# Two gate tiles moved from attention into the stick breaking, and one gate's sigmoid written as exp and reciprocal

## The chip, the cores and the metric

The kernel runs on one core of a Trainium2 chip. The metric is the time of one execution in microseconds, device time. A time without a profile is a median of runs; a profile is one further execution, and its numbers are compared with that execution's own time.

The core has five engines that work side by side, each through its own list of instructions in order: PE (matrix products and transposes), DVE and ACT (element by element work, ACT also functions such as exp), POOL (element by element work) and SP, which here only issues loads and stores. An instruction waits for the ones whose results or whose buffers it needs, and everything behind it on its engine waits with it.

## What is computed

Two layers of a model over 512 tokens with 1024 features. Each layer has a mixer and a convolutional feed-forward part, each between two normalizations and added to the stream. The change touches the mixer:

```python
def hybrid_mixer(h, positions, w_in, ...):
    q_nsa, kv_nsa, g_nsa, qkv_sb, g_merge = jnp.split(h @ w_in, cuts, axis=-1)
    ...
    o_nsa = nsa_attention(...)
    o_sb = stick_breaking_attention(qkv[:, :, 0], qkv[:, :, 1], qkv[:, :, 2]).reshape(B, T, SB_WIDTH)
    g_a, g_b = jnp.split(jax.nn.sigmoid(g_merge), 2, axis=-1)
    y = g_a * (o_nsa @ w_proj_nsa) + g_b * (o_sb @ w_proj_sb)
    return y @ w_out

def stick_breaking_attention(q, k, v):
    ...
        z = jnp.einsum('bqhd,bkhd->bhqk', q[:, q0:q1], k[:, :q1]).astype(jnp.float32) * scale
        log_1m = jnp.where(strict, -jax.nn.softplus(z), 0.0)
        later = lax.cumsum(log_1m, axis=3, reverse=True) - log_1m
        w = jnp.where(strict, jnp.exp(jax.nn.log_sigmoid(z) + later), 0.0)
        outs.append(jnp.einsum('bhqk,bkhd->bqhd', w.astype(v.dtype), v[:, :q1]))
```

So the mixer needs, from one large product with `w_in`, the inputs of two attentions, and two gates of 1024 features each, `g_a` and `g_b`. The gates are used only after the attentions.

## The kernel before

Activations lie with features on the 128 partitions and tokens along the columns. Every number of a product is split into a high and a low part, and a product of 512 columns is three matmuls per 128 features (high with high, low with high, high with low): one output tile of 128 features is 24 matmuls, called a **tile of filling** here. Its weights come from a fixed list of items (`Weights`, in the order of the `it(...)` calls): SP loads an item into one of three raw buffers, ACT copies its high part (`whi`, L119), and DVE or POOL, as the item says, subtracts to get the low part (`wlo`, L123). `get` takes the next item, so the order of the list must be that of the tiles.

A mixer runs in two stages that matter here.

**Attention** (L888 to L1067). 32 pairs of head and query block (`Sub`) go through scores `S` on PE, maximum and small reciprocal on DVE (`st`, L955, L970, L971), exp on ACT (`P`), scaling on POOL (L974), transposes on PE (`tp`, L985, two banks), evacuation of the transposed weights as high part by ACT (`pt`, L994) and low part by DVE (L996), and the product with the values (`pv`). Behind these the program has the filling: four tiles for the queries and keys of the first two pairs of stick-breaking heads (`sb_pair`), eight tiles of the gate `ga` (`gate`, each evacuated by DVE at L849), and four tiles of values (`sb_values`: a tile, four transposes at L868 and an evacuation). A planner puts these matmuls among attention's instructions by its own estimates of durations; the result is fixed before the kernel runs. The filling has one accumulation bank here (`f`).

**Stick breaking** (L1073 to L1194). Eight heads, each in three steps: `s` (scores into a bank `Z`, then Abs, Exp, Relu, Ln on ACT and four scans and a subtraction on DVE), `t` (Exp on ACT, ten transposes on PE, high part `wh` by ACT, low part `wl` by DVE), `p` (product with the values, then `pvl` on ACT and `o_s` on DVE, which frees `Z`, of which there are two). The order of PE's work is written out in `SB_ORDER`: `s3` is step s of head 3, and each `f` takes the next piece of `filling()`: the last four tiles of `sb_pair`, eight tiles of the gate `gb`, and eight projections of attention's output of 12 matmuls each, multiplied into `ga` at L1162. PE keeps exactly that order (`chained`); the filling alternates between two banks, `f` and `g`.

Before the stick breaking both halves of `ga` go through a sigmoid:

```python
            for i in range(2):
                act(ga[i], ga[i], AF.Sigmoid)
```

`act` loads a function table (L268) whenever the function is of another set than the last one. Exp and Ln are in one set, Sigmoid is in another. The two halves of `gb` go through Sigmoid after the stick breaking in the program's text.

Of the kernel before, what the change touches and what calls it, by code (L numbers as in the profile page):

```python
# [13 lines left out]
AF = mybir.ActivationFunctionType  # L14
OP = mybir.AluOpType
# [20 lines left out]
SB_H = 8  # L36

SB_ORDER = ("s0 f s1 f f t0 f p0 f s2 t1 f p1 f s3 t2 f p2 f s4 t3 f p3 f s5 t4 f p4 f s6 "
            "t5 f f p5 f s7 t6 f f p6 f t7 f p7")

ALL = slice(0, T)
HALVES = (slice(0, HT), slice(HT, T))
# [148 lines left out]
def run_kernel(ctx, tc, xT, pos, inv, vec, pew, cw1, w_m, w_vn, w_pr, w_o, w_u, w_d, xmid, rot, out):  # L191
    nc = tc.nc
    uid = [0]

    def nm(s):
        uid[0] += 1
        return f"{s}_{uid[0]}"
# [11 lines left out]
    def hold(tag):  # L209
        return lambda i: held["slot"](tag, f"wh{i}", FR)  # L210
# [3 lines left out]
    def it(ap, n=1024, dest=None, eng=nc.vector, fold=0):  # L214
        items.append((ap, n, dest, eng, fold))

    for l in range(DEPTH):
        for i in range(HEAD):
            it(w_m[l, i], dest=hold(("sa", "sb", "vs0", "vs1")[i - 2]) if i >= 2 else None, eng=nc.vector)
        for c, n, k in ((0, 840, "q1"), (840, 840, "on"), (1680, 560, "sa")):  # L220
            it(w_vn[l, :, c:c + n], n, dest=hold(k))
        it(w_m[l, 6])
        it(w_m[l, 7])
        for v in range(2):
            it(cw1[l, :, v * 1024:(v + 1) * 1024], dest=hold(("vs0", "vs1")[v]), fold=16)
        for i in list(range(8, 12)) + list(range(16, 24)) + list(range(32, 36)):
            it(w_m[l, i], eng=nc.vector if i in (8, 9, 10) else nc.gpsimd)
        for i in list(range(12, 16)) + list(range(24, 32)):
            it(w_m[l, i])
        for i in range(8):  # L230
            it(w_pr[l, i])
        for i in range(8):
            it(w_o[l, i], dest=hold(("q0", "k0", "k1", "vs1")[i - 2]) if 2 <= i < 6 else None)
        for i in range(2 * NF):
            it(w_u[l, i], dest=hold(("sa", None, None, "q0", "k0", "k1")[i]) if i in (0, 3, 4, 5) else None)
        dts = list(range(8 - TAIL_D)) + 2 * list(range(8 - TAIL_D, 8))
        for j, i in enumerate(dts):
            k0 = 0
            for c, n in enumerate(DCH):
                keep = i == KEPT and c < 2  # L240
                if not (keep and j >= 8):
                    it(w_d[l, i, :, k0 * 128:(k0 + n) * 128], n * 128,
                       dest=(Strips(lambda: h_hi, 4 * c), Strips(lambda: h_lo, 4 * c)) if keep else None)
                k0 += n
# [7 lines left out]
    def after(op, earlier):  # L252
        tc.add_manual_dep(op.ins, earlier.ins.name,
                          mybir.DependencyInfo(mybir.DependencyClass.NoSync, mybir.DependencyReason.DATA),
                          reason="order of issue")

    def act(out_, in_, fn, **kw):


        load_table(fn)  # L260
        op = nc.scalar.activation(out_, in_, fn, **kw)  # L261
        after(op, table["load"])
        table["users"].append(op)

    def load_table(fn):
        name = SETS.get(fn, fn)
        if name != table["set"]:
            load = nc.scalar.preload_act_table_set(name) if isinstance(name, str) else nc.scalar.preload_act_table(fn)  # L268
            for op in table["users"]:
                after(load, op)  # L270
            table.update(set=name, load=load, users=[])
# [154 lines left out]
    def fbank(name):  # L426
        return ps1.tile([128, T], F, name=nm(name), tag="f" if name == "f" else "g", bufs=1)

    def gemm(o, wt, rhi, rlo, kts, first=True, last=True, woff=0, step=6, ahead=None):

        hi, lo = wt
        n = 0
        for j, kt in enumerate(kts):
            c = (woff + j) * 128
            a = hi[:, c:c + 128]
            b = lo[:, c:c + 128]
            f = first and j == 0
            e = last and j == len(kts) - 1
            for w_, r_, f_, e_ in ((a, rhi(kt), f, False), (a, rlo(kt), False, False), (b, rhi(kt), False, e)):
                mm(o, w_, r_, f_, e_)  # L440
                n += 1
                if n % step == 0 and not (e_ and last):
                    yield
        if ahead is not None:
            W.ensure(W.n_got - 1 + ahead)
        yield

    def drain(g, side=None):
        for _ in g:
            if side is not None:  # L450
                side.tick()

    def h_of(tr):
        return (lambda kt: h_hi[:, kt, tr]), (lambda kt: h_lo[:, kt, tr])
# [111 lines left out]
    for l in range(DEPTH):  # L566
# [8 lines left out]
        def slot(k, name, dt=F):  # L575
            return rp.tile([128, SLOT], dt, name=nm(name), tag=k)
# [236 lines left out]
        def fill_bank():  # L813
            fills[0] += 1
            return fbank("fg"[fills[0] % fills[1]])

        def sb_pair(p, st):

            st = st.rearrange("p (a e t) -> p a e t", a=2, e=2)
            qlo = rp.tile([128, T], FR, name=nm("qlo"), tag="qlo", bufs=4)  # L820
            for t in range(2):
                b = fill_bank()
                drain(gemm(b, W.get(), *h_of(ALL), range(KD), ahead=2))
                with tc.high_priority():
                    z = rp.tile([128, T], F, name=nm("sbz"), tag="sbz")
                    nc.vector.scalar_tensor_tensor(z, b, 0.125 if t == 0 else 1.0, r2, op0=OP.mult, op1=OP.mult)  # L826
                    for e in range(2):
                        r = slice(e * 64, e * 64 + 64)
                        ro = slice(64 - e * 64, 128 - e * 64)
                        d = st[:, t, e]  # L830
                        nc.scalar.copy(d[r], z[r])
                        if t == 0:
                            nc.sync.dma_start(d.bitcast(F)[ro], d.bitcast(F)[r])
                        nc.vector.tensor_sub(qlo[r] if t == 0 else d[ro], z[r], d.bitcast(F)[r])
                if t == 1:
                    sbq[p] = (st[:, 0], qlo, st[:, 1])
                yield

        ga, gb = {}, {}
        at = lambda s, k: s[k // 4][:, (k % 4) * T:(k % 4) * T + T]  # L840

        def gate(dst, half, tag):

            dst[half] = slot(tag, "gate")
            for m in range(4 * half, 4 * half + 4):
                b = fill_bank()
                drain(gemm(b, W.get(), *h_of(ALL), range(KD), ahead=2))
                with tc.high_priority():
                    nc.vector.tensor_mul(at(dst, m), b, r2)  # L849
                yield  # L850
# [6 lines left out]
        def sb_values():  # L857

            vS.extend([slot("q0", "vS0", FR), slot("k0", "vS1", FR)])
            for c in range(4):  # L860
                b = fill_bank()
                drain(gemm(b, W.get(), *h_of(ALL), range(KD), ahead=2))
                z = rp.tile([128, T], F, name=nm("sbz"), tag="sbz")
                with tc.high_priority():
                    nc.vector.tensor_mul(z, b, r2)
                tp = fbank("f")
                for j in range(4):
                    nc.tensor.transpose(tp[:, j * 128:(j + 1) * 128], z[:, j * 128:(j + 1) * 128], ident)  # L868
                with tc.high_priority():
                    src = tp.rearrange("p (j h c) -> p h j c", j=4, h=2)  # L870
                    v4 = vS[c // 2].rearrange("p (h j c) -> p h j c", h=4, j=4)[:, c % 2 * 2:c % 2 * 2 + 2]
                    nc.scalar.copy(v4[:, :, :, 0:64], src)
                    nc.vector.tensor_sub(v4[:, :, :, 64:128], src, v4.bitcast(F)[:, :, :, 0:64])
# [14 lines left out]
        with temps(0) as nt, pool("pn", space=PSUM) as pn:  # L888
# [173 lines left out]
                    pv_pair(pv_due.pop(0))  # L1062
            drain(sb_pair(0, slot("sa", "sbst", FR)))
            drain(sb_pair(1, slot("sb", "sbst", FR)))
            drain(gate(ga, 0, "vs0"))
            drain(gate(ga, 1, "vs1"))
            sb_values()  # L1067

# [2 lines left out]
        with temps(3) as sw, pool("pz", space=PSUM) as pz:  # L1073
# [91 lines left out]
            def filling():  # L1165
                yield from sb_pair(2, slot("vn", "sbst", FR))
                yield from sb_pair(3, sw.tile([128, SLOT], FR, name=nm("sbst")))
                yield from gate(gb, 0, "k1")
                yield from gate(gb, 1, "sa")
                yield from projection_n()  # L1170

            for i in range(2):
                act(ga[i], ga[i], AF.Sigmoid)
            heads = [Head(h) for h in range(SB_H)]
            fill = filling()
            fills[1] = 2
            chained[0] = True
# [253 lines left out]
```

## Time and profile before

| what | value |
|---|---|
| median of 3 runs | 1635.32 us (1633.79 to 1635.38) |
| the profiled execution | 1636.58 us, its span 1634.9 us |
| granted TensorE clock, mean | 0.985 |
| ACT_TABLE_LOAD (L268) | 20, 1283 ns each |
| first layer: scores S, and Z | 80.9 to 219.2 us, 245.3 to 382.2 us |
| second layer: scores S, and Z | 886.3 to 1024.3 us, 1050.7 to 1187.8 us |

The two layers run the same program in these stages, so one layer is read closely and counted twice. The views used are: the page's head with each engine's busy time; windows, which give the busy time of each engine in stretches of the span, with the clock that PE was granted; the waits of one engine, by what ended them; the chain of waits, followed back from the last instruction, in order of time; and rows of groups of like instructions with their mean durations. A matmul's own duration (0.39 us for 512 columns) overlaps the next one; what a tile of filling costs PE is read from the chain, where the pieces follow each other.

### The profile page before, as it was taken

How to read it: one execution, taken by the hardware profiler on the slowest of the kernel's cores; microseconds unless marked ns; L12 is line 12 of the kernel's file. 1: busy time of each engine (PE TensorE's matmuls, PEld its weight loads, DVE VectorE, ACT ScalarE, POOL GpSimd, SP SyncE). 2: the span in 40 equal slices, each digit the busy share in tenths (PEclk: the TensorE clock that was granted, in tenths of full speed). 3: DMA queues.
4: the chain of work that ended last, by engine and by line, in shares of the span. 5: the costliest groups of instructions: out<-in, count | busy, mean ns of one | idle time of the engine just before them, and what ended most of it. 6: DMA issues, size and time to landing. Idle time of an engine off the chain costs nothing. (4 is left out here: it accounts for less than half of the span.)

```text
span 1634.9 us, 23009 instructions
## 1 busy us (share of the span) xinstructions
PE 1585.0 (97%) x8874; PEld 1372.3 (84%) x8874; DVE 1095.1 (67%) x1671; ACT 887.9 (54%) x1412; POOL 182.8 (11%) x298
## 2 busy tenths in 40 slices
PE   9999999998999999999999999999799999999997
PEld 8878878876998888888998888787689988888897
DVE  8876666676578777733688766577576687776235
ACT  6865567664545444423568555666735454444232
POOL 0056440000000000000000655200000000000000
PEclk9999999998999999999999999999999999999999
DMA  6321112213412232333563211121143133323343
GB/s 224 115 75 43 53 39 91 65 52 116 142 53 91 90 104 90 100 94 112 170 201 88 72 40 52 43 89 64 51 168 103 40 103 93 101 95 93 98 129 119
DMA packets 50238, 153.66 MB, mean 94 GB/s; under 512 B 5584, under 2 KB 11216, under 8 KB 50128
## 3 DMA queue, kind: packets, MB, share of 16 engines
q1 hardware_dynamic: 47824, 146.23, 28.2%
q0 software_dynamic: 1296, 4.72, 0.8%
q8 instruction: 70, 1.15, 0.3%
q10 hardware_dynamic: 1008, 1.23, 0.3%
q14 instruction: 40, 0.33, 0.1%
HBM read 142.20 MB, written 4.72 MB: 90 GB/s over the span
## 5 line engine op out<-in xcount | busy, mean ns | idle before, releaser
L119 ACT CAST whi<-wraw 128x1024 fp32r<-128x1024 f32 (+2 forms) x227 | 233.1, 1028 | 307.0 <-PE bk L424 243.0
L123 DVE TENSOR_TENSOR wlo<-wraw,whi 128x1024 fp32r<-128x1024 f32 (+2 forms) x201 | 238.8, 1189 | 189.4 <-ACT whi L119 186.6
L424 PE MATMUL bk<-h_hi,wlo 128*128 128x512 f32 (+1 forms) x736 | 277.2, 377 | 0.0
L424 PE MATMUL bk<-h_hi,whi 128*128 128x512 f32 (+1 forms) x736 | 275.9, 375 | 0.6 <-ACT whi L119 0.6
L424 PE MATMUL bk<-h_lo,whi 128*128 128x512 f32 (+1 forms) x736 | 276.1, 375 | 0.0
L424 PE MATMUL f<-h_lo,whi 128*128 128x512 f32 (+1 forms) x416 | 163.5, 393 | 0.0
L424 PE MATMUL f<-h_hi,whi 128*128 128x512 f32 (+1 forms) x384 | 152.9, 398 | 7.5 <-DVE sbz L826 5.9
L424 PEld LDWEIGHTS bk<-h_hi,whi 128*128 128x128 f32 x736 | 138.3, 188 | 26.0 <-ACT whi L119 0.8
L424 PEld LDWEIGHTS bk<-h_hi,wlo 128*128 128x128 f32 x736 | 138.4, 188 | 25.3
L424 PEld LDWEIGHTS bk<-h_lo,whi 128*128 128x128 f32 x736 | 138.4, 188 | 24.7
L424 PE MATMUL f<-h_hi,wlo 128*128 128x512 f32 (+1 forms) x384 | 149.4, 389 | 0.0
L424 PE MATMUL bk<-ah,wlo 128*128 128x512 f32 (+1 forms) x420 | 142.6, 340 | 0.5 <-DVE wlo L123 0.5
L424 PE MATMUL bk<-ah,whi 128*128 128x512 f32 (+1 forms) x420 | 142.3, 339 | 0.0
L424 PE MATMUL bk<-al,whi 128*128 128x512 f32 (+1 forms) x420 | 142.2, 338 | 0.0
L974 POOL TENSOR_TENSOR P<-P,st 128x256 f32<-128x256 f32 x160 | 94.4, 619 | 108.8 <-DVE st L971 56.3
L1296 DVE TENSOR_TENSOR cu<-bk,r 128x512 f32<-128x512 f32 x88 | 60.2, 688 | 61.1 <-PE bk L424 60.9
L424 PE MATMUL bk<-h_hi,wh 128*128 128x256 f32 x512 | 95.9, 284 | 0.0
L424 PEld LDWEIGHTS f<-h_lo,whi 128*128 128x128 f32 x416 | 81.0, 195 | 13.1
L424 PEld LDWEIGHTS f<-h_hi,whi 128*128 128x128 f32 x384 | 73.8, 192 | 21.1 <-DVE sbz L826 6.3
L996 DVE TENSOR_TENSOR pt<-tp,pt 128x512 fp32r<-128x512 f32 (+1 forms) x96 | 56.3, 595 | 49.0 <-ACT pt L994 39.9
L424 PEld LDWEIGHTS bk<-ah,wlo 128*128 128x128 f32 x420 | 79.6, 190 | 9.4 <-DVE wlo L123 0.7
L424 PEld LDWEIGHTS bk<-ah,whi 128*128 128x128 f32 x420 | 79.7, 190 | 8.7
(261 smaller groups left out, 3384.1 us busy)
## 6 DMA issues: line engine op xcount, KB each, us to landing
wraw<-in_w_u SPq DMA_DIRECT2D x88, 512.0 KB, 3.5
wraw<-in_w_m SPq DMA_DIRECT2D x72, 512.0 KB, 3.3
wraw<-in_w_d SPq DMA_DIRECT2D x40, 512.0 KB, 3.5
wraw<-in_w_d SPq DMA_DIRECT2D x22, 384.0 KB, 3.0
wraw<-in_w_pr SPq DMA_DIRECT2D x16, 512.0 KB, 3.5
wraw<-in_w_o SPq DMA_DIRECT2D x16, 512.0 KB, 3.6
wraw<-in_cw SPq DMA_DIRECT2D x4, 512.0 KB, 3.7
kst<-kst SPq DMA_DIRECT2D x8, 256.0 KB, 3.4
```

What stands on the lines that cost most here:

```text
L119: self.nc.scalar.copy(hi[:, c], raw[:, c])
L123: eng.tensor_sub(lo[:, s], raw[:, s], hi.bitcast(F)[:, s])
L424: queue(nc.tensor.matmul(o, a, b, start=first, stop=last, skip_group_check=True))
L974: nc.gpsimd.tensor_mul(pv[:, j], pv[:, j], st[:, 2:4, None].to_broadcast([128, 2, 128]))
L996: nc.vector.tensor_sub(lo[:, :w_, self.hm], src, hi.bitcast(F)[:, :w_, self.hm])
L1296: nc.vector.tensor_mul(u, b, r2)
```

## The change

Attention's filling keeps six of the eight tiles of `ga`: two of the first half, then the values, then the other two of the first half and two of the second. The last two tiles of `ga` become pieces of the stick breaking's filling, after `sb_pair`. `SB_ORDER` has 22 `f` instead of 20, the new ones towards the end. The sigmoid of `ga` becomes `logistic`: Exp of the negative on ACT, then plus one and reciprocal on DVE, in place. The first half goes through it before the stick breaking, the second after its last tile. `gb` keeps its Sigmoid. The weights' list follows the new order; of the eight items of `ga` the six of attention's filling have POOL for the low part, and the last two DVE.

```diff
@@ SB_ORDER @@
-            "t5 f f p5 f s7 t6 f f p6 f t7 f p7")
+            "t5 f p5 f f s7 t6 f f p6 f f t7 f f p7")
@@ the items @@
-        for i in list(range(8, 12)) + list(range(16, 24)) + list(range(32, 36)):
+        for i in list(range(8, 12)) + [16, 17] + list(range(32, 36)) + list(range(18, 22)):
             it(w_m[l, i], eng=nc.vector if i in (8, 9, 10) else nc.gpsimd)
-        for i in list(range(12, 16)) + list(range(24, 32)):
+        for i in list(range(12, 16)) + list(range(22, 32)):
             it(w_m[l, i])
@@ behind attention @@
-            drain(gate(ga, 0, "vs0"))
-            drain(gate(ga, 1, "vs1"))
+            g0, g1 = gate(ga, 0, "vs0"), gate(ga, 1, "vs1")
+            next(g0)
+            next(g0)
             sb_values()
+            drain(g0)
+            next(g1)
+            next(g1)
@@ filling() of the stick breaking @@
                 yield from sb_pair(3, sw.tile([128, SLOT], FR, name=nm("sbst")))
+                yield from g1
+                logistic(ga[1])
                 yield from gate(gb, 0, "k1")
@@ ahead of the stick breaking @@
-            for i in range(2):
-                act(ga[i], ga[i], AF.Sigmoid)
+            def logistic(g):
+
+                act(g, g, AF.Exp, scale=-1.0)
+                nc.vector.tensor_scalar(g, g, 1.0, None, op0=OP.add)
+                nc.vector.reciprocal(g, g)
+
+            logistic(ga[0])
```

In the changed kernel the lines from L1063 on are shifted (L1126 is L1130, L1140 is L1144, L1151 is L1155, L1162 is L1166).

**Attention's tail on DVE**, second layer. `st` is a pair's maximum and its reciprocal, `pt<-tp,pt` the low part that frees a bank of transposes, `sbz` and `vS` belong to the values. Before:

```order
L996 TENSOR_TENSOR pt_9255<-tp_9302,pt_9254 128x2x128
L970 RECIPROCAL st_9340<-st_9340 128x2
L971 TENSOR_TENSOR st_9340<-st_9340,gates_7490 128x2
L873 TENSOR_TENSOR vS_1045_9948<-f_10029,vS_1045_9948 128x8x64
L996 TENSOR_TENSOR pt_9337<-tp_9326,pt_9336 128x4x128
L996 TENSOR_TENSOR pt_9339<-tp_9331,pt_9338 128x4x128
L970 RECIPROCAL st_9392<-st_9392 128x2
L971 TENSOR_TENSOR st_9392<-st_9392,gates_7490 128x2
```

And now, at the same pair of head and block (`gate_9662` is the first half of `ga`, `gate_9977` the second):

```order
L996 TENSOR_TENSOR pt_9251<-tp_9298,pt_9250 128x2x128
L970 RECIPROCAL st_9336<-st_9336 128x2
L971 TENSOR_TENSOR st_9336<-st_9336,gates_7486 128x2
L1181 TENSOR_SCALAR gate_9662<-gate_9662 128x2048
L1182 RECIPROCAL gate_9662<-gate_9662 128x2048
L996 TENSOR_TENSOR pt_9333<-tp_9322,pt_9332 128x4x128
L970 RECIPROCAL st_9388<-st_9388 128x2
L849 TENSOR_TENSOR gate_9977<-f_9978,r_90 128x512
```

Between the product of one pair and the low parts of the pair before it now stand the addition and the reciprocal over 128x2048. PE's list goes on, at that place, with the rest of a tile into bank f and then the transposes of the next pair, which go into the bank that `pt_9333<-tp_9322` frees.

**Attention's tail on ACT.** Before, a table load stands on each side of the two sigmoids, ahead of `pvl` and of the high parts `pt`:

```order
L261 ACTIVATE P_9402,st_9392<-S_9355,st_9392 128x4x128 x2
L268 ACT_TABLE_LOAD
L261 ACTIVATE gate_9666<-gate_9666 128x2048
L261 ACTIVATE gate_9807<-gate_9807 128x2048
L268 ACT_TABLE_LOAD
L1018 COPY pvl_9378<-pv_9361 64x256
L994 CAST pt_9336<-tp_9382 128x4x128
```

Now:

```order
L261 ACTIVATE P_9346,st_9336<-S_9316,st_9336 128x4x128 x2
L261 ACTIVATE gate_9662<-gate_9662 128x2048
L994 CAST pt_9332<-tp_9322 128x4x128
L261 ACTIVATE P_9398,st_9388<-S_9351,st_9388 128x4x128 x2
L994 CAST pt_9334<-tp_9327 128x4x128
L1018 COPY pvl_9374<-pv_9357 64x256
```

One Exp of the gate is left there, one pair earlier, and no load.

**The middle of the stick breaking on DVE.** `wl` is a head's low part (here of head 2), `sbr` the scans of head 3, `gate_10359` and `gate_10401` the first half of `gb`. Before:

```order
L1151 TENSOR_TENSOR o_s_10118<-Z_10194,pvl_10471 64x512
L849 TENSOR_TENSOR gate_10359<-g_10474,r_90 128x512
L123 TENSOR_TENSOR wlo_10500<-wraw_10340,whi_10499 128x1024
L1140 TENSOR_TENSOR wl_10542<-Z_10392,wh_10541 128x1280
L849 TENSOR_TENSOR gate_10359<-f_10545,r_90 128x512
L123 TENSOR_TENSOR wlo_10571<-wraw_10389,whi_10570 128x1024
```

Now:

```order
L1155 TENSOR_TENSOR o_s_10044<-Z_10119,pvl_10395 64x512
L1181 TENSOR_SCALAR gate_9977<-gate_9977 128x2048
L849 TENSOR_TENSOR gate_10401<-g_10402,r_90 128x512
L1182 RECIPROCAL gate_9977<-gate_9977 128x2048
L123 TENSOR_TENSOR wlo_10428<-wraw_10265,whi_10427 128x1024
L1144 TENSOR_TENSOR wl_10470<-Z_10316,wh_10469 128x1280
L849 TENSOR_TENSOR gate_10401<-f_10473,r_90 128x512
L123 TENSOR_TENSOR wlo_10499<-wraw_10313,whi_10498 128x1024
```

The second half's addition and reciprocal stand around a gate product, ahead of head 2's `wl`.

## The prediction

> **What bounds the kernel now.** The page's head and engine shares come first.
>
> ```profile
> span 1634.9 us, 23009 instructions
> PE 1585.0 (97%) x8874; PEld 1372.3 (84%) x8874; DVE 1095.1 (67%) x1671; ACT 887.9 (54%) x1412; POOL 182.8 (11%) x298
> ```
>
> PE is taken 97% of the span, so only two things move the time: PE work that goes, which this change hardly has, and the waits between PE's instructions. To find those I cut the second layer in four (the window view: length, then busy time of PE, PEld, DVE, ACT, POOL, granted clock): attention up to its last score block, attention's tail, the stick breaking until head 4 is out, and its end.
>
> ```profile
> 886.30:1024.30 138.00, 134.30 (x787) 113.08 (x785) 93.69 (x213) 81.71 (x211) 78.44 (x121) 0.99 0.16 54
> 1024.30:1050.70 26.40, 24.30 (x148) 21.01 (x145) 13.80 (x26) 17.46 (x27) 7.28 (x12) 0.94 0.11 41
> 1050.70:1140.10 89.40, 88.95 (x456) 73.79 (x455) 62.88 (x74) 63.88 (x66) 0.00 (x0) 1.00 0.23 77
> 1140.10:1187.70 47.60, 37.87 (x178) 30.60 (x176) 29.22 (x34) 29.37 (x26) 0.00 (x0) 0.89 0.15 45
> ```
>
> PE is full in the first and third stretch, and idle 9.7 us at the end of the stick breaking, where the clock drops as well. Who ends those waits, in the view of PE's waits from 1040 to 1190 (total, times, longest):
>
> ```profile
> PE Z L424 <- DVE wl L1140: 3.9, 2, 3.4
> PE Z L1136 <- ACT sbt L261: 3.7, 2, 2.8
> PE Z L424 <- DVE o_s L1151: 2.6, 2, 2.2
> ```
>
> All three are a head's softmax chain that PE has too little filling to cover. The chain of waits shows attention's tail (start, length):
>
> ```profile
> 1029.22 1.28 ACT L268
> 1030.52 3.14 ACT gate L261 x2
> 1034.26 1.28 ACT L268
> 1035.94 0.59 ACT pt L994
> 1037.40 1.09 PE tp L985 x4
> ```
>
> Two table loads and two sigmoids hold the evacuation of transposed weights there. So there is something to gain in both places; the question is what the new instructions on DVE cost. The prices, from the same chain, are those of one tile of filling, of a head's scores, its transposes, its output, and of half a tile (a projection):
>
> ```profile
> 1066.23 5.44 PE g L424 x24
> 1058.96 1.61 PE Z L424 x12
> 1071.67 1.09 PE Z L1136 x10
> 1078.27 1.17 PE Z L424 x8
> 1152.76 2.76 PE g L424 x12
> ```
>
> **The new DVE operations.** Each layer gets two reciprocals and two additions over 128x2048. The trace has reciprocals of 2 and of 16 columns only (min/median/max ns), and products of 16, 512 and 1024 columns:
>
> ```profile
> L970 DVE RECIPROCAL st<-st x64: 149/158/168, 89.6 to 1029.2; 128x2 f32<-128x2 f32 x64
> L913 DVE RECIPROCAL cm<-cm x4: 243/248/256, 108.7 to 973.3; 128x16 f32<-128x16 f32 x4
> L916 DVE TENSOR_TENSOR cm<-cm,gates 128x16 f32<-128x16 f32 x4 | 0.7, 168 | 0.0
> L1296 DVE TENSOR_TENSOR cu<-bk,r 128x512 f32<-128x512 f32 x88 | 60.2, 688 | 61.1 <-PE bk L424 60.9
> L123 DVE TENSOR_TENSOR wlo<-wraw,whi 128x1024 fp32r<-128x1024 f32 x177 | 216.4, 1223 | 144.6 <-ACT whi L119 141.9 <-PE bk L424 0.5
> L364 DVE TENSOR_SCALAR rt_n<-rt_ang 128x512 f32<-128x512 f32 x3 | 1.3, 422 | 0.0
> ```
>
> A product costs (1223 - 688)/512 = 1.045 ns a column, and at 16 columns still only 168 ns. The reciprocal takes 158 ns at 2 columns and 248 at 16, thus 90/14 = 6.4 ns a column. The bounds for 2048 columns: at the product's rate 0.15 + 2.14 = 2.3 us; by the widest reading of the two rows, (256 - 149)/14 = 7.6 ns a column, 15.8 us. I take the middle of the reciprocal's own rows, the nearest there are: 0.158 + 2046 x 6.43 ns = **13.3 us**. [...] The addition is 0.15 once and four times 0.27 (the 422 ns row less 0.15): 1.2 us, at most 4 x 0.422 = 1.7.
>
> **Attention's filling.** Two tiles leave it: -10.9 us. Three groups of four transposes (L868, 4 x 0.095 us) that stood behind the last score block come before it: +1.1. PE was busy 134.3 of 138 us here, while DVE had 93.7 and ACT 81.7, so I count the whole as shorter: **-9.8**. The two sides: all of it, or none (+1.1) if the chain of one head pair is already as long as PE's work; the loads of DVE and ACT, 68% and 59%, stand nearer to all.
>
> **Attention's tail.** Time 0 is the end of the last score block (1024.3 before; Z then began at 26.4). DVE does the maximum (1.2), the small reciprocal and product, all out by 2.4. ACT runs Exp on the gate by 3.4; it is the shape of the sigmoid:
>
> ```profile
> L261 ACT ACTIVATE gate<-gate x8: 1892/1905/1921, 225.4 to 1179.3; 128x2048 f32<-128x2048 f32 x8
> ```
>
> DVE adds by 4.6 and is in the reciprocal from 4.6 to 17.9. Queued behind it stand the subtraction `pt<-tp,pt` that frees a transpose bank (0.7), the last head's small reciprocal, the gate product that frees PE's bank f, and two more. PE meanwhile has 24 matmuls (5.44), two groups of transposes (0.44 each) and a pv (2.3): 8.6. Then its next transposes need the bank, at 18.7: a wait of **10.1 us** that wasn't there. Behind it are 24 matmuls, six groups of transposes (2.6) and two pv (4.6), 12.7; bank f and the last evacuation, some 1.8; and the clock, 1.8. The last is the price of a wait before:
>
> ```profile
> 1145.31 2.23 PE Z L424 x12
> 1147.54 2.32 PE Z L1136 x10
> ```
>
> After 2.2 us of idleness these took 0.62 and 1.23 more than the rows 1.61 and 1.09. Z starts at 18.7 + 16.3 = 35.0: **+8.6**. This includes what the sigmoids and the loads took (2.1 us of PE's idleness), which goes; what is late next is the reciprocal.
>
> **The stick breaking.** Until head 4 is out it has as many tiles as before, less one group of transposes: -0.4. But the second reciprocal stands in it, behind the gate product of the tile g. From that tile's end PE has scores 1.61, transposes 1.09 and a tile 5.44: 8.1. Then it needs `wl` (L1140 before). DVE is through the gate product at 1.2, the reciprocal at 14.5, a weight's subtraction (1.22) at 15.7, `wl` at 17.2; behind that stand the next gate product, head 3's scans and head 2's `o_s`, and PE comes to none of them before `wl`:
>
> ```profile
> L1140 DVE TENSOR_TENSOR wl<-Z,wh 128x1280 fp32r<-128x1280 f32 x16 | 23.8, 1488 | 33.5 <-ACT wh L1139 33.5
> ```
>
> A wait of 9.1 and a slow clock of 1.8: **+10.9**. DVE's 62.9 of 89.4 us let it catch up with the rest. The gate's Exp, 1.9 us, lies in ACT's idle time there (63.9 of 89.4 busy), while DVE still works on head 2; without that cover it would push each later step by 1.9.
>
> **Its end.** Two more tiles' worth lie between the outputs. Before head 6's scores now stand 5.44 instead of 2.76 (wait 2.2 gone), before head 7's 5.5 instead of 2.76 (0.4 gone). Before head 6's transposes the work since its scores hardly changes (14.8 us), and 0.4 of the 0.9 stays. Before head 7's it was 10.6 us of work and waits of 0.9 and 2.8, a chain of 14.3; now it is 13.3 of work, and some 1.3 stay with the slow clock. Before the last output ACT still has its order of loads and sigmoids of gb:
>
> ```profile
> 1176.22 1.28 ACT L268
> 1177.51 0.19 ACT gate L261
> ...
> 1179.33 1.90 ACT gate L261
> 1181.25 1.28 ACT L268
> 1182.54 1.24 ACT wh L1139
> 1183.80 1.50 DVE wl L1140
> 1185.35 2.52 PE Z L424 x8
> ```
>
> From the transposes' start that was 9.1 us, now with one weight's copy ahead 10.1, against 6.6 of PE's work: 3.5 us stay. Adding up from head 4's output: two tiles 10.9, eight projections 22.0, scores twice 3.2, transposes three times 3.3, outputs 4.9 (the last at 2.5): 44.3, waits 0.4 + 1.3 + 3.5: about 49.6 for 47.6: **+2.0**, though 10.9 us of work came in.
>
> No other edit costs: the loads of weights are as many and as large, two subtractions per layer go from POOL to DVE (1.22 each), into DVE's idle third; without that cover they would cost 2.4. A weight whose subtraction waits behind the reciprocal keeps its raw buffer and so SP's next load; that is 3.3 us to landing, with three buffers, and stays behind the same wait.
>
> **Sum:** -9.8 + 8.6 - 0.4 + 10.9 + 2.0 = +11.3 per layer, +22.6 for two. The profiled execution took 1636.6 us (span 1634.9 and 1.7 around it), 1.3 above the median 1635.3; so 1659.2 against its own time, and **1658** against the median.
>
> **Rivals.** (1) *The reciprocal runs at a product's rate*, 2.3 us. Both waits go, since PE's 8.6 and 8.1 us cover them: the tail ends at 8.6 + 12.7 + 1.3 = 22.6 (-3.8), the sum -9.8 - 3.8 - 0.4 + 2.0 = -12.0 per layer, 1611 us. It decides below a price of 7.7 us, since each microsecond counts twice per layer (13.3 - 11.3/2). For it speaks that no large one is in the trace; against it both small rows. [...] (3) *Attention doesn't get shorter*, since its chain takes over: up to +10.9 per layer, 1680; a third gives 1665. Against it DVE's and ACT's loads. (4) *The waits are covered* by half, as PE or DVE come to them at other moments than I place them: 1638 to 1642. That the tiles don't move isn't open: the order shows it.
>
> **How the numbers follow.** My forecast 0.55 (1648 to 1664), rival 1 0.15, rival 2 0.15, rival 3 0.07, rival 4 0.08, half of which is within 0.2%. About 0.2% is what a measurement of this kernel can tell from no change. Faster 0.16, same 0.04, slower 0.80. The range 1640 to 1680 leaves out rival 1 and a part of rival 4.
>
> **What would show it.** [...] PE should wait some 10 us per layer for `pt` L996 in attention's tail, and some 9 for `wl` in the middle of the stick breaking; attention up to its last score block should be near 128 us, the end from head 4's output near 50. If the reciprocal is short, or attention stays at 138, I am wrong there.

## The result, and the profile after

The changed kernel took 1655.87 us (median of 4 runs, 1655.19 to 1658.21), the kernel before beside it 1634.55 us (4 runs, 1630.99 to 1635.38). The ratio is 1.0131, 95% interval 1.0118 to 1.0143: **slower**, by 21.3 us or 1.3%, with the whole interval above 1. The profiled execution took 1655.42 us, 18.8 more than the profiled execution before (1636.58), which lay 2.0 above its own median. The head of its page and its engine shares:

```profile
span 1653.7 us, 22991 instructions
PE 1582.9 (96%) x8874; PEld 1371.7 (83%) x8874; DVE 1152.7 (70%) x1683; ACT 882.5 (53%) x1408; POOL 172.6 (10%) x282
```

PE's busy time is about what it was (1585.0), with the same 8874 matmuls, in a span that is 18.8 us longer. So the time went into PE's waits. DVE has 57.6 us more work. The second layer in the same four stretches as before (length, busy time of PE, PEld, DVE, ACT, POOL, granted clock):

```profile
895.00:1026.50 131.50, 127.08 (x752) 106.92 (x752) 93.31 (x216) 81.55 (x214) 72.29 (x113) 0.97 0.15 49
1026.50:1060.60 34.10, 22.90 (x136) 19.69 (x136) 27.10 (x25) 11.80 (x22) 8.47 (x13) 0.85 0.14 47
1060.60:1159.20 98.60, 90.26 (x453) 75.11 (x452) 73.17 (x70) 65.36 (x66) 0.00 (x0) 0.95 0.20 65
1159.20:1207.40 48.20, 44.81 (x226) 36.86 (x224) 35.53 (x42) 31.44 (x28) 0.00 (x0) 0.98 0.21 66
```

Attention got shorter, and the end took in two tiles of filling (226 matmuls for 178) and grew by only 0.6 us. But PE is now idle for 11.2 us of attention's tail and for 8.3 us of the stick breaking's first part, where it was idle for 2.1 and 0.45 before. PE's waits from 895 to 1212 (total, times, longest) name the two:

```profile
PE Z L424 <- DVE wl L1144: 11.7, 2, 8.3
PE tp L985 <- DVE st L970: 10.1, 1, 10.1
PE f L424 <- DVE sbz L826: 3.0, 1, 3.0
```

The new operations themselves, among the instructions of the gate's tiles (min/median/max ns):

```profile
L1181 DVE TENSOR_SCALAR gate<-gate x4: 1227/1362/1507, 212.8 to 1108.7; 128x2048 f32<-128x2048 f32 x4
L1182 DVE RECIPROCAL gate<-gate x4: 12942/12948/12953, 214.3 to 1110.4; 128x2048 f32<-128x2048 f32 x4
```

The chain of waits leads through both reciprocals. In attention's tail (start, length):

```profile
1031.24 4.07 DVE gate L1182
1035.31 8.80 issue
1044.11 0.63 DVE pt L996
1044.74 0.08 DVE st L970
1044.82 0.07 issue
1044.89 1.09 PE tp L985 x4
```

And in the middle of the stick breaking:

```profile
1110.42 7.20 DVE gate L1182
1117.62 5.66 issue
1123.28 1.16 DVE wlo L123
1124.44 1.41 DVE wl L1144
1125.85 0.04 issue
1125.89 2.50 PE Z L424 x8
```

The piece "issue" behind each L1182 is the rest of that reciprocal: 4.07 + 8.80 and 7.20 + 5.66 are 12.9 us each. Behind the first one PE's transposes wait for the bank that `pt` L996 frees (the waits view names `st` L970, the small instruction that ended last); behind the second, head 2's output waits for `wl`.

### The profile page after: what moved, and what is told of

Read it like the earlier page. It is cut to its first block, busy times and chain, and to the rows that moved or that the text cites. A ratio compares the mean times of both kernels' runs of the same rounds, so it can differ in the third digit from the quotient of the medians.

```text
span 1653.7 us, 22991 instructions
## 1 busy us (share of the span) xinstructions
PE 1582.9 (96%) x8874; PEld 1371.7 (83%) x8874; DVE 1152.7 (70%) x1683; ACT 882.5 (53%) x1408; POOL 172.6 (10%) x282
## 5 line engine op out<-in xcount | busy, mean ns | idle before, releaser
L123 DVE TENSOR_TENSOR wlo<-wraw,whi 128x1024 fp32r<-128x1024 f32 (+2 forms) x205 | 243.5, 1189 | 178.8 <-ACT whi L119 176.7
L424 PEld LDWEIGHTS bk<-h_hi,whi 128*128 128x128 f32 x736 | 138.4, 188 | 25.6 <-ACT whi L119 0.6
L424 PE MATMUL f<-h_lo,whi 128*128 128x512 f32 (+1 forms) x400 | 156.6, 391 | 0.0
L424 PE MATMUL f<-h_hi,whi 128*128 128x512 f32 (+1 forms) x368 | 148.6, 404 | 5.5 <-DVE sbz L826 4.4
L424 PE MATMUL f<-h_hi,wlo 128*128 128x512 f32 (+1 forms) x368 | 144.0, 391 | 0.0
L994 ACT CAST pt<-tp 128x512 fp32r<-128x512 f32 (+1 forms) x96 | 49.2, 517 | 81.1 <-PE tp L985 71.0
```

The costliest lines, as they stand in the source:

```text
L123: eng.tensor_sub(lo[:, s], raw[:, s], hi.bitcast(F)[:, s])
L424: queue(nc.tensor.matmul(o, a, b, start=first, stop=last, skip_group_check=True))
L994: nc.scalar.copy(hi[:, :w_, self.hm], src)
```

## The experiments

The theory was: three terms stand side by side. Moving two tiles out of attention gains; each reciprocal is a block in DVE's list, and PE pays for the part of it that its own work does not cover; the loads of ACT's tables matter little. The rivals: the moved tiles themselves cost; the loads are the gain; DVE's load, not the place of the block, is what costs. Every variant was timed against the kernel before on the same chip (1634.2 to 1635.6 us).

**The two halves of the change, each alone.** First the moved tiles with the old Sigmoid:

```diff
             def logistic(g):
-                act(g, g, AF.Exp, scale=-1.0)
-                nc.vector.tensor_scalar(g, g, 1.0, None, op0=OP.add)
-                nc.vector.reciprocal(g, g)
+                act(g, g, AF.Sigmoid)
```

> The two tiles stay moved, as in the changed kernel, but ga's gate is a Sigmoid on ACT again, without exponential, addition and reciprocal. My theory: the shorter attention is worth 6.5 to 11 us per layer and stays; both waits behind the reciprocals (10.2 and 8.3 us of PE per layer) go; back come the loads of ACT's tables, two in the attention's tail and two more at the second Sigmoid within the stick breaking, 1.3 us each, with a Sigmoid of 1.9 us. Sum: 1612 to 1625 us. Rival, that the changed kernel's loss comes from the moved tiles themselves: 1640 or more. Second rival, that the loads of tables cost far more than their own time because scores wait for ACT: 1625 to 1635.

Measured: 1615.58 us (1613.23 to 1617.17), ratio 0.9874, interval 0.9858 to 0.9891. Its second layer in the four stretches:

```profile
874.50:1004.60 130.10, 125.68 (x752) 105.88 (x752) 93.25 (x216) 81.39 (x214) 72.19 (x112) 0.99 0.15 49
1004.60:1028.90 24.30, 21.79 (x137) 18.56 (x137) 13.14 (x23) 14.43 (x24) 7.55 (x13) 1.00 0.20 66
1028.90:1117.70 88.80, 88.31 (x452) 73.40 (x452) 59.39 (x68) 67.78 (x68) 0.00 (x0) 1.00 0.23 72
1117.70:1165.00 47.30, 43.92 (x224) 36.17 (x223) 35.70 (x42) 31.42 (x28) 0.00 (x0) 1.00 0.20 65
```

Attention is as short as in the changed kernel, and the other three stretches are no longer than before. So the moved tiles are worth 20 us, and the move costs nothing elsewhere. Then the new sigmoid alone, in the kernel before:

```diff
-            for i in range(2):
-                act(ga[i], ga[i], AF.Sigmoid)
+            for g in (ga[0], ga[1]):
+                act(g, g, AF.Exp, scale=-1.0)
+                nc.vector.tensor_scalar(g, g, 1.0, None, op0=OP.add)
+                nc.vector.reciprocal(g, g)
```

> The kernel before, with the two tiles and the table of order unmoved, and only ga's Sigmoids replaced by exponential, addition and reciprocal. My theory: a reciprocal of 12.95 us costs what waits behind it on DVE wherever it stands; here both stand in the middle of the attention, where DVE's work on the scores is waited for, and no tile moves to pay for it: two blocks of 8 to 12 us per layer against 2 to 4 us for the loads saved: 1645 to 1675 us, likeliest 1660. Rival, that a reciprocal in the attention is hidden behind the filling, because PE has other matmuls at hand there: 1627 to 1634.

Measured: 1675.06 us (1671.58 to 1678.49), ratio 1.0246, interval 1.0221 to 1.0271, at the upper end of what was expected, and 15 us above its likeliest value. Both reciprocals stand in attention here, which takes 156.5 us for 138.0 in the second layer; the stretch and PE's waits from 905 to 1225:

```profile
905.90:1062.40 156.50, 137.07 (x791) 116.06 (x790) 120.51 (x218) 85.95 (x215) 80.48 (x120) 0.95 0.15 49
```

```profile
PE pv L424 <- DVE pt L996: 10.3, 2, 9.4
PE tp L985 <- DVE pt L996: 5.5, 2, 5.0
```

So a block in attention is not hidden behind the filling: PE has its list in a fixed order and stops at the transposed weights. In the profiled executions the span grew by 35.0 us (1634.9 to 1669.9), and the 18.0 and 18.5 us of the two layers' attention account for all of it. Of what was expected back from the missing loads, 2 to 4 us per layer, attention's tail got only 0.5 and 0.8 us shorter. The four kernels together:

| | old Sigmoid | exp, addition, reciprocal |
|---|---|---|
| tiles where they were | 1635.6 | 1675.1 (+39.5) |
| two tiles moved | 1615.6 (-20.0) | 1655.9 (+21.3) |

Each difference is taken against the kernel before beside it (1634.55 for the changed kernel, 1635.57 for the other two). The two halves nearly add up (-20.0 + 39.5 = +19.5, for +21.3), though the blocks stand in other places in the two kernels of the right column.

**The sigmoid without DVE, and without loads.** In the changed kernel, 1 / (1 + exp(-x)) as three passes of functions that are in one set:

```diff
                 act(g, g, AF.Exp, scale=-1.0)
-                nc.vector.tensor_scalar(g, g, 1.0, None, op0=OP.add)
-                nc.vector.reciprocal(g, g)
+                act(g, g, AF.Ln, bias=1.0)
+                act(g, g, AF.Exp, scale=-1.0)
```

> The changed kernel with the sigmoid of both halves of ga as three passes on ACT (Exp, Ln with bias 1, Exp of the negative; one table set, no load), nothing on DVE; everything else as changed. Theory (the reciprocals hold DVE's list, and PE waits behind them in two places of each layer, 10.1 and 8.3 us, plus a slow clock): both waits go, attention's tail of the second layer from 34.1 us to 23 to 25, the stick breaking until head 4's output from 98.6 to 88 to 90, and the time is 1608 to 1620. Rival (moving the two tiles thins out attention's filling, and this costs the time): the waits only change hands and the time stays above 1635.

Measured: 1618.69 us (1617.98 to 1620.01), ratio 0.9895, interval 0.9879 to 0.9911, as expected: both big waits go with the reciprocals. The stick breaking until head 4 is out, however, took 92.7 and 91.1 us in the two layers, and not the 88 to 90 expected: the passes on ACT cost something there. The same three lines in the kernel before, tiles unmoved:

> The kernel before, with the two tiles and the table of order unmoved, and only ga's Sigmoids in the tail replaced by an exponential, a logarithm (with 1 added in the same pass) and an exponential on ACT. My theory: only the loads of tables and the Sigmoids in the tail go, some 2 to 4 us per layer, and the six ACT passes now stand in the attention: 1627 to 1631 us. Rival, that moving the tiles brings nothing and the whole gain of the variant with both (1618.7 us) is the missing loads: 1617 to 1621.

Measured: 1635.91 us (10 runs, 1633.83 to 1639.47), ratio 1.0006, interval 0.9995 to 1.0017. Neither the theory's 1627 to 1631 nor the rival's 1617 to 1621: taking two loads and two Sigmoids per layer out of the tail and putting six passes on ACT in their place brings nothing in sum. What the loads alone are worth isn't shown by this, but the rival that they are the gain falls. The variant with the Sigmoid above agrees: it has 24 loads, and its median is 3 us below that of the three passes with the tiles moved, which have 16 (the intervals of the two ratios overlap). Their rows of table loads, in this order:

```profile
L268 ACT ACT_TABLE_LOAD x24 | 30.8, 1283 | 1.2 <-PEq L1428 0.8
```

```profile
L268 ACT ACT_TABLE_LOAD x16 | 20.5, 1283 | 1.1 <-PEq L1430 0.8
```

**One reciprocal at a time.** In the changed kernel only the half named keeps addition and reciprocal; the other half takes the three passes on ACT (the first variant is shown; the second has `False` for `True`):

```diff
-                act(g, g, AF.Exp, scale=-1.0)
-                nc.vector.tensor_scalar(g, g, 1.0, None, op0=OP.add)
-                nc.vector.reciprocal(g, g)
+                if (g is ga[0]) == True:
+                    act(g, g, AF.Exp, scale=-1.0)
+                    nc.vector.tensor_scalar(g, g, 1.0, None, op0=OP.add)
+                    nc.vector.reciprocal(g, g)
+                else:
+                    act(g, g, AF.Exp, scale=-1.0)
+                    act(g, g, AF.Ln, bias=1.0)
+                    act(g, g, AF.Exp, scale=-1.0)
```

> The first half of ga (attention's tail) keeps addition and reciprocal on DVE, the second half (stick breaking) goes through the three passes on ACT. Theory: the tail's wait of 10.1 us stays, the 8.3 us for wl in the stick breaking goes with its slow clock, 9 to 10 us per layer: 1635 to 1638. By my own terms the tail's reciprocal should be the dearer one (12.4 against 10.9 per layer). Rival (DVE's added load counts wherever it stands): half of what both reciprocals cost, whichever half is kept.

Measured: 1646.30 us (1641.56 to 1646.65), ratio 1.0056, interval 1.0036 to 1.0077: above the range of 1635 to 1638, and above the rival's half of what both cost, some 1637.

> The reverse: first half on ACT, second half keeps addition and reciprocal on DVE. Theory: the tail's wait goes, 34.1 us becomes 23 to 25; the 8.3 us for wl in the middle of the stick breaking stays: 1631 to 1636. With the run before this one and the one without reciprocals, the two costs should add up to that of both.

Measured: 1632.59 us (10 runs, 1631.33 to 1636.42), ratio 0.9984, interval 0.9974 to 0.9995: as expected. The waits over the whole span, of the first variant and then of the second, show that each reciprocal has its own wait and keeps it unchanged without the other:

```profile
PE tp L985 <- DVE st L970: 20.3, 2, 10.2
```

```profile
PE Z L424 <- DVE wl L1144: 23.4, 4, 8.3
```

Against the three passes (1618.7) the first reciprocal costs 27.6 us and the second 13.9, together 41.5, where both at once cost 37.2. In the profiled runs the first lengthens attention's tail from 23.4 to 34.0 us in both layers, which is 21 of the 27.6. Most of the rest is no part of the block: layer 1's attention took 131.4 us for 127.0, with a wait for `sbz` at its beginning of 3.0 us for 1.4 (that half clock behind this wait makes up the other 2.8 us is my estimate, from the variant with `gb` too below: after the same wait of 3.0 us the granted clock was 0.71 from 80 to 90 us there, which loses 2.9), and the stick breaking of layer 2 took 2.8 more. Those 4.4 us, which come before any reciprocal and which layer 1 of the changed kernel doesn't have, are also about the size of what the two costs have too much. The second is the cheaper one here in part because the passes on ACT that replace it cost something too: the stick breaking's first part takes 91 to 94 us with them in these profiles, and 88.8 with the Sigmoid.

**Block or load.** Now the first half takes the three passes, and the second half's reciprocal is cut into four pieces of 512 columns, one behind each second tile of `gb`, held there by a dependence on that tile's product, which `last_gate` keeps (shown in part: the addition of the second half stays one instruction):

```diff
-                yield from gate(gb, 0, "k1")
-                yield from gate(gb, 1, "sa")
+                for m, (half, tag) in enumerate(((0, "k1"), (1, "sa"))):
+                    for n, _ in enumerate(gate(gb, half, tag)):
+                        if n % 2 == 0:
+                            c = slice((2 * m + n // 2) * T, (2 * m + n // 2) * T + T)
+                            after(nc.vector.reciprocal(ga[1][:, c], ga[1][:, c]), last_gate[0])
+                        yield
...
```

> As the run before (first half on ACT, second half reciprocal on DVE), but the reciprocal in four pieces of 512 columns, one behind every second gate tile, so one per head instead of one block. DVE has the same work. Theory (it is the block in DVE's list, not its load): a piece of 3.3 us fits into the 4.4 us per head in which DVE idles, wl is no longer late by 8.3 us, and the time is within 4 us of the kernel without reciprocals. Rival (load): the time is that of the run with one block, 1631 to 1636.

Measured: 1613.83 us (1611.57 to 1616.49), ratio 0.987, interval 0.985 to 0.9891: 18.8 us faster than the same work in one block, and in the median even 4.9 below the three passes. Its pieces, PE's waits over the whole span, and the stretch of the second layer in which three of its four pieces stand (the fourth begins at 1120.6):

```profile
L1179 DVE RECIPROCAL gate<-gate x8: 3341/3343/3344, 282.8 to 1120.6; 128x512 f32<-128x512 f32 x8
```

```profile
PE Z L424 <- DVE wl L1145: 8.7, 6, 3.3
```

```profile
1025.50:1114.30 88.80, 88.35 (x453) 73.48 (x452) 69.96 (x72) 65.21 (x66) 0.00 (x0) 1.00 0.23 72
```

DVE does 69.96 us there for 73.17 in the changed kernel, one piece less, and the 8.3-us wait is gone; the 3.3 that is left is head 7's, as before. As a control, the changed kernel with each reciprocal cut into four pieces that stay in a row:

```diff
-                nc.vector.reciprocal(g, g)
+                for c in range(4):
+                    nc.vector.reciprocal(g[:, c * T:c * T + T], g[:, c * T:c * T + T])
```

> The changed kernel, with each reciprocal cut into four of 512 columns that are issued one behind the other at the same place. Control for the variant with spaced pieces (1613.8 us): if cutting alone were what helped there, this would be near 1614 to 1635. My theory: only the place in DVE's order counts, and four pieces in a row are the same block: 1653 to 1660 us.

Measured: 1657.59 us (1657.21 to 1658.11), ratio 1.0142, interval 1.0121 to 1.0164, with the waits of the changed kernel:

```profile
PE Z L424 <- DVE wl L1144: 23.4, 4, 8.4
PE tp L985 <- DVE st L970: 20.4, 2, 10.2
```

So cutting does nothing by itself; it is what stands between the pieces. The load of DVE as a rival falls. Spacing was tried for the second half alone; whether attention's tail would take the first half's pieces as well isn't shown.

**The length of the block.** Only half the columns, which leaves the other half of the gate at 1 + exp:

```diff
-                nc.vector.reciprocal(g, g)
+                nc.vector.reciprocal(g[:, :2 * T], g[:, :2 * T])
```

> The changed kernel, with the reciprocal taken over the first 1024 of the gate's 2048 columns only; the other columns are left as 1 + exp, so that half of the gate isn't inverted. This prices a block of about 6.5 us in place of 12.95. My theory: each microsecond of the block beyond what PE has at hand counts fully, twice per layer, so both waits shrink by 6.4 us, to some 3.7 and 1.9, with slower matmuls behind the first: 1626 to 1636 us, likeliest 1631, near the kernel before; by the prediction's break-even price of 7.7 us it would be 1630. Rival, that the wait is a matter of order and not of length, so that half a block keeps much of it: 1640 to 1650. Rival, that a block this short is wholly covered: 1614 to 1620.

Measured: 1629.23 us (10 runs, 1627.16 to 1632.33), ratio 0.9972, interval 0.9959 to 0.9985. The reciprocal, and the waits from 880 to 1180:

```profile
L1182 DVE RECIPROCAL gate<-gate x4: 6541/6549/6555, 214.0 to 1089.1; 128x1024 f32<-128x1024 f32 x4
```

```profile
PE Z L424 <- DVE wl L1144: 5.3, 2, 3.3
PE tp L985 <- DVE st L970: 3.8, 1, 3.8
```

The block is 6.40 us shorter, and so is the first wait (10.1 to 3.8); of the `wl` row 3.3 belongs to head 7, so the second went from 8.3 to 2.0. The time fell by 26.6 us, and four blocks times 6.4 are 25.6: between these two lengths each microsecond of a block counts fully, twice per layer, as the prediction's break-even had it (1630 for this length).

**The end of the stick breaking.** The three passes for `ga` as above, and `gb` by the same passes as soon as each half is there, in place of the late Sigmoids:

```diff
                 yield from gate(gb, 0, "k1")
+                logistic(gb[0])
                 yield from gate(gb, 1, "sa")
+                logistic(gb[1])
...
-            for i in range(2):
-                act(gb[i], gb[i], AF.Sigmoid)
```

> As the variant with exponential, logarithm and exponential for ga (1618.7 us), and gb's Sigmoids, which stand at the stick breaking's end and load two tables there, are replaced in the same way, as soon as each half of gb is there within the stick breaking. My theory: the loads and the Sigmoid at the end go from the path, 3 to 5 us per layer, and two more ACT blocks of 5.8 us stand within the stick breaking, which cost 0 to 3 us each: 1606 to 1622 us, likeliest 1613. Rival, that the end isn't waiting for ACT: 1619 to 1630.

Measured: 1623.15 us (1621.36 to 1625.01), ratio 0.9922, interval 0.9905 to 0.9938: above the theory's range, within the rival's, and no better than without it (1618.69). In the profiled runs the end got shorter by 1.3 and 1.8 us (47.8 and 48.3 to 46.5), so it did wait for ACT, but for less than the 3 to 5 us expected, and the stick breaking's first part gave as much back (92.7 and 91.1 to 94.1 and 92.9). Layer 1's attention was 4.5 longer: its wait for `sbz` took 3.0 us for 1.4, and the granted clock was 0.71 from 80 to 90 us and 0.95 from 90 to 100, for 1.00 in both without the passes for `gb`. Layer 2's was 1.4 shorter, with a wait of 2.9 us in both; what made it shorter wasn't shown. So nothing shows the passes for `gb` to be slower either. The step from the end's wait to a gain was wrong.

**The fastest of all the kernels here** is thus the move of the tiles alone, with the Sigmoid left as it was (1615.58), or with the spaced reciprocal (1613.83); their intervals overlap, so nothing here ranks these two.

## Why the prediction was right

The forecast was 1658, measured were 1655.87. The mechanism was right: two long reciprocals, two new waits of PE behind named instructions, and an attention whose gain doesn't pay for them. That the sum came so near is in part luck: per layer attention's gain was smaller than forecast by almost 2 us, the middle of the stick breaking and its end were cheaper by about 1 and 1.5, and the two layers, which the forecast took for equal, grew by 7.4 and 11.0 us for a forecast 11.3. Its steps against the stretches of the profiled executions, in microseconds per layer (forecasts were made on layer 2):

| step | forecast | layer 1 | layer 2 |
|---|---|---|---|
| one reciprocal | 13.3 | 12.95 | 12.95 |
| attention up to the last score block | -9.8 | -11.2 | -6.5 |
| attention's tail | +8.6 | +8.5 | +7.7 |
| its new wait | 10.1 | 10.2 | 10.1 |
| stick breaking until head 4 is out | +10.5 | +9.6 | +9.2 |
| its new wait | 9.1 | 8.3 | 8.3 |
| its end | +2.0 | +0.5 | +0.6 |

**The price of the reciprocal** carried everything. The slope between two rows of 2 and 16 columns, 6.43 ns a column, held to 2048 columns within 3%: 12.95 us are 6.25 ns a column. Rival 1 (a product's rate, 2.3 us) is out by this row alone. The price of a column behind rival 2's 0.15 is shown by no run; what the runs showed is 6.25 ns, six times a product's 1.045.

**The two waits** came where the order put them, behind the instructions that were named, at 10.1 and 8.3 us. The 1.8 us that the forecast added for the slow clock behind each wait hold as well: in the second layer the half clock lasted 3.5 us behind the first and 4.4 behind the second, half of which is 1.8 and 2.2. That each microsecond of price counts 4 us in all was shown by the half block, between 6.55 and 12.95 us.

**Attention's gain** was over-priced by almost 2 us, and the layers hid it. Rival 3, that it doesn't get shorter, is out: with the Sigmoid the move is worth 20 us. The layers differ by a wait that the forecast did not treat, that for `sbz` at attention's start, and by the half clock behind it. In layer 1 the wait was 3.1 us before and 1.5 after, with 3.4 us of half clock before and none after; in layer 2 it was 2.8 and 3.0, with 3.4 and 6.2 us of half clock. At half clock half of the time is lost (14 matmuls for 29 in the same 6.2 us, last section). Without these differences layer 1 gives -11.2 + 1.6 + 1.7 = -7.9 and layer 2 -6.5 - 0.2 - 1.4 = -8.1, for -9.8. In the move with the Sigmoid, where the clock is the same 0.99 as before, PE's busy time fell by 8.6 us (134.30 to 125.68) and not by the 9.8 that I had counted, and its idle time rose by 0.7 (3.7 to 4.4). Why 35 records fewer make only 8.6 us wasn't settled.

**The end** was over-priced: the 1.3 us that I kept before head 7's transposes, and the 0.4 before head 6's, don't appear among PE's waits of the changed kernel; only the 3.4 us before the last output stays, forecast as 3.5.

**The loads of tables** were counted as 2.1 us of idleness that goes from the tail. The variant that keeps Sigmoid has a tail of 24.3 us against 23.4 with the passes that need no load, so going without them is worth 0.9 there, less than half of what was counted; with the tiles unmoved, the passes in their place gained nothing in the whole time (1635.91).

Rival 4, that the waits are half covered, is out as well: 10.1 of 10.1 us and 8.3 of 9.1 came.

## What to carry to other kernels

Price an operation that the trace shows only at small sizes by the slope between its own rows, not by its neighbours' rate. A long instruction on an engine that is only two thirds busy can still stop everyone who waits for what is queued behind it (12.95 us on DVE, busy 70% of the span, made PE wait 10.1 and 8.3): compare its length with the work that the waiting engine has at hand at that place, and if it is longer, cut it and put the pieces between the others' work; cutting alone did nothing here. And time the halves of a change apart: here one half was worth -20 us and the other +39.5.

## What the runs showed of the hardware

The reciprocal's time was linear in its columns: 3.30 us at 512 (in a row), 6.55 at 1024, 12.95 at 2048, the last two 6.25 ns a column apart.

PE's clock after a wait was the surprise. The same wait for `sbz` (DVE's evacuation of a tile of `sb_pair`), 2.95 us long, was followed by two different clocks. In the changed kernel (start, length of each matmul of the second layer's first tile):

```profile
898.87 0.80 PE L424 MATMUL f<-h_hi,whi 128*128 128x512 f32 x1 [2.95 <-DVE sbz L826]
899.47 0.63 PE L424 MATMUL f<-h_lo,whi 128*128 128x512 f32 x1
899.89 0.63 PE L424 MATMUL f<-h_hi,wlo 128*128 128x512 f32 x1
```

And in the kernel with the spaced reciprocal:

```profile
877.35 0.50 PE L424 MATMUL f<-h_hi,whi 128*128 128x512 f32 x1 [2.95 <-DVE sbz L826]
877.69 0.40 PE L424 MATMUL f<-h_lo,whi 128*128 128x512 f32 x1
877.92 0.39 PE L424 MATMUL f<-h_hi,wlo 128*128 128x512 f32 x1
```

The windows of the 6.2 us behind both, busy times and then the granted clock, first of the changed kernel:

```profile
898.80:905.00 6.20, 6.13 (x14) 4.85 (x15) 3.95 (x11) 5.42 (x13) 0.61 (x1) 0.50 0.46 127
```

and of the other:

```profile
877.30:883.50 6.20, 6.15 (x29) 5.13 (x29) 4.31 (x11) 5.95 (x14) 0.61 (x1) 1.00 0.45 127
```

14 matmuls in the one and 29 in the other: about 3 us lost or not, by something that the wait's length does not decide. In the changed kernel the half clock lasted 6.2 us after this wait of 2.95, and 3.5 us after the one of 10.1. The kernel before shows it after shorter waits too. PE's wait of 2.2 us that ended at 1145.3 is followed, two microseconds on, by this window:

```profile
1147.30:1149.30 2.00, 2.00 (x11) 1.88 (x11) 0.00 (x0) 1.72 (x2) 0.00 (x0) 0.50 0.00 0
```

What differs is where the wait lies. A trace lists the granted clock with its changes. In the kernel before and in the changed one the stretches of half clock start on a fixed grid of 3.41 us, and all but the last of each trace are one to three such steps long. In the changed kernel 2.31 of the wait's 2.95 us lie in one step, and half clock starts at that step's end:

```profile
894.82:898.23 3.41, 1.10 (x8) 0.71 (x6) 2.91 (x10) 2.47 (x4) 0.00 (x0) 1.00 0.00 0
898.23:901.64 3.41, 2.77 (x7) 2.21 (x8) 2.66 (x6) 3.35 (x6) 0.00 (x0) 0.50 0.23 44
```

In the kernel with the spaced reciprocal, on the grid of its own half-clock stretches, the same wait is split between two steps, and the clock stays whole:

```profile
872.07:875.48 3.41, 2.33 (x14) 1.70 (x12) 2.94 (x8) 1.25 (x2) 0.00 (x0) 1.00 0.16 64
875.48:878.89 3.41, 1.54 (x7) 1.28 (x8) 3.31 (x9) 3.35 (x6) 0.00 (x0) 1.00 0.00 0
```

In the traces of the kernel before and of the changed one, PE was busy for at most 41.5% of a step at full clock 19 times, and half clock followed each time; of the 905 busier steps it followed one, busy for 49.7%. The wait of 2.2 us before 1145.3 left its step, 1143.21 to 1146.63, busy for 1.32 of 3.42 us.

The wait and what follows it go with the same instructions at attention's start being 4 us longer or shorter between variants (127.1 us in layer 1 of the changed kernel, 131.4 with the first reciprocal alone), which is as much as some of the effects that the profiles were compared for.
